# A mixed attention and state-space encoder on one core: the last pass of a score tile, rotary query times the low part of the rotary key, on all 128 rows in place of 64

## The chip, the core and the metric

The kernel runs on one core of a Trainium2 chip. A core has five engines with queues of their own: TensorE (PE in the rows, its weight loads PEld), VectorE (DVE), ScalarE (ACT), GpSimd (POOL) and SyncE (SP), which here issues all DMAs. The metric is device time in microseconds (us) of one execution, the median of several.

## The reference

Two post-norm layers over 512 tokens of width 1024. The even layer has a convolution branch, a latent attention with 8 heads and a cross-attention into 256 memory tokens; the odd layer has a bidirectional state-space branch and the same cross-attention. The change lies in the scores of the latent attention: each head has 128 plain channels and 64 rotary ones, and the rotary key is shared by all heads.

```python
def mla_block_attention(q_nope, q_rope, k_nope, k_rope, v):
    scale = (QK_NOPE + QK_ROPE) ** -0.5
    ...
        s = (jnp.einsum('bqhd,bkhd->bhqk', qn_b, k_nope).astype(jnp.float32)
             + jnp.einsum('bqhr,bkr->bhqk', qr_b, k_rope).astype(jnp.float32)) * scale
        p = jax.nn.softmax(s, axis=-1).astype(v.dtype)
        return jnp.einsum('bhqk,bkhd->bqhd', p, v)
```

## The kernel before, in words

Matrix products run in fp32r. To keep the accuracy of fp32, every operand is split into a high part (a cast to fp32r on ScalarE) and a low part (operand minus high part, on VectorE), and a product is the sum of three passes on TensorE: high times high, low times high, high times low. The helper `split_into` makes the two parts, `mm3` issues the passes.

The kernel is not written in the order in which it runs. The functions record every operation through one helper (so nearly all instructions have line 535 in the profile, and the tile names tell them apart: `sr` holds fp32r tiles in SBUF, `sb` and `sz` fp32 ones, `ps` is PSUM, `scr` is scratch in DRAM). A list scheduler then sets a fixed order for each engine, with a cost table of its own: priorities follow the recorded order, and work marked as background (the 31 taps of the convolution on VectorE, the preparation of the state-space parameters on GpSimd, VectorE and TensorE) is put into gaps. Each engine runs its order strictly, and waits on semaphores where an operand or a buffer isn't ready.

A head of the latent attention, `mla_head(h)`: it splits the weights, makes the key (`kh`, `kl`) and the query (`qh`, `ql`), and for each pair of heads the rotary query. That one is stacked: the tile `st` of a head holds in 64 rows the high part and in the other 64 rows the low part. The shared rotary key (`krh`, `krl`) stands twice in its tile, in rows 0 to 63 and again in 64 to 127, so one pass of `st` times `krh` on 128 rows gives high times high plus low times high. For each of four score tiles (128 queries by 512 keys, one PSUM bank `s`) there are five passes: three for the plain channels, one with `krh`, one with `krl`. VectorE takes the row maximum (`reduce_max`), ScalarE the exponential with the row sum, VectorE the reciprocal, ScalarE the scaling; TensorE transposes the probabilities, ScalarE and VectorE split them, and TensorE multiplies them with the values. With 8 heads there are 32 score tiles.

Around the heads the order on TensorE mixes in passes of other projections and small products of the state-space preparation, on VectorE the taps of the convolution. Behind the heads come the output projection (weights `wo`), and then the odd layer.

Of the kernel before, what the change touches and what calls it, by code (L numbers as in the profile page):

```python
# [537 lines left out]
class Kernel:  # L538
# [361 lines left out]
    def mla_head(self, h):  # L900
        nc, A = self.nc, self.A
        if h % 4 == 0:
            self.v = self.mla_v(h // 4)
        wkn = self.wload(A["wkn"][h], 256, tag="k")
        ckv = [(t[0][:], t[1][:]) for t in self.ckv]
        cqa = lambda k: (self.cq[k][0][:], self.cq[k][1][:])
        ps = self.bank("A")
        self.mm3(ps[:], [self.wk(wkn, k) for k in range(2)], ckv)
        kh, kl = self.split(ps[:])
        ps = self.projF(A["wqn"][h], cqa, 6)  # L910
        qh, ql = self.split(ps[:])
        if h % 2 == 0:
            ps = self.projF(A["wqr"][h // 2], cqa, 6)
            r = self.rope(ps)
            self.stk = []
            for i in range(2):
                st = self.big(F32R)
                a, b = slice(i * 64, i * 64 + 64), slice((1 - i) * 64, (1 - i) * 64 + 64)
                nc.scalar.copy(st[a], r[a])
                nc.vector.tensor_tensor(st[b], r[a], st[a].bitcast(F32), op=ALU.subtract)  # L920
                self.stk.append(st)
        i = h % 2
        st = self.stk[i]
        rows = slice(i * 64, i * 64 + 64)
        scale = 192.0 ** -0.5
        pr = []
        for t in range(4):
            sl = slice(t * P, (t + 1) * P)
            s = self.bank("S")
            nc.tensor.matmul(s[:], lhsT=qh[:, sl], rhs=kh[:], start=True, stop=False)  # L930
            nc.tensor.matmul(s[:], lhsT=ql[:, sl], rhs=kh[:], start=False, stop=False)
            nc.tensor.matmul(s[:], lhsT=qh[:, sl], rhs=kl[:], start=False, stop=False)
            nc.tensor.matmul(s[:], lhsT=st[:, sl], rhs=self.krh[:], start=False, stop=False)
            nc.tensor.matmul(s[:], lhsT=st[rows, sl], rhs=self.krl[rows], start=False, stop=True)
            mx = self.sm(1, tag="mx")
            nc.vector.reduce_max(mx[:], s[:], axis=AX.X)
            p = self.big(F32, "pr")
            self.softmax_tail(s[:], p[:], scale, mx[:])
            pr.append(p)
        pt = []  # L940
        for k in range(4):
            tp = self.bank("T")
            for t in range(4):
                nc.tensor.transpose(tp[:, t * P:(t + 1) * P], pr[t][:, k * P:(k + 1) * P], self.ident[:])
            pt.append(self.split(tp[:]))
        o = self.bank("V")
        vs = slice((h % 4) * P, (h % 4) * P + P)
        self.mm3(o[:], [(v[0][:, vs], v[1][:, vs]) for v in self.v], [(a[:], b[:]) for a, b in pt])
        m = self.tmp()
        nc.sync.dma_start(out=m[:], in_=self.mgd[h][:])  # L950
        nc.vector.scalar_tensor_tensor(m[:], o[:], 0.5, m[:], op0=ALU.mult, op1=ALU.mult)
        return m
# [671 lines left out]
```

## Time and profile before

| | |
|---|---|
| timed runs, us | 1058.15, 1063.86, 1064.89; median 1063.86 |
| profiled execution, us | 1060.0 |
| its span, first to last instruction, us | 1058.2 |
| busy us: TensorE, VectorE, ScalarE, GpSimd | 1007.6, 799.2, 450.1, 514.7 |
| mean granted TensorE clock | 0.979 |

The profiled execution lies among the timed ones, so its durations can be used as they are. Matmuls overlap in the rows: the duration of one is longer than the step to the next.

### The profile page before, as it was taken

To read this page: it belongs to the slowest core of one execution; us is meant where nothing else is said; L and a number is where in the kernel's file an instruction comes from. 1 tells how busy PE (TensorE), PEld (TensorE's weight loads), DVE (VectorE), ACT (ScalarE), POOL (GpSimd) and SP (SyncE) were. 2 spreads that over 40 slices of the span, in tenths; PEclk is the share of its full clock that TensorE was granted. 3 is DMA by queue.
4 is the path that set the end of the run, shared out by engine and by line. 5 is a ranking of instruction groups with operands and counts; after the bars stand their busy time and mean duration, and the time that the engine had idled before them with its cause. 6 is when DMAs were issued, how large, how long until landed. Compare 5 with 4: busy or idle time off the path is not lost. (4 is left out here: it accounts for less than half of the span.)

```text
span 1058.2 us, 15020 instructions
## 1 busy us (share of the span) xinstructions
PE 1007.6 (95%) x5296; PEld 792.2 (75%) x5296; DVE 799.2 (76%) x1285; ACT 450.1 (43%) x798; POOL 514.7 (49%) x741
## 2 busy tenths in 40 slices
PE   9999899999999999998799999999989979999996
PEld 7888788787788666665578888887767757888885
DVE  7787999999999898987896648517797695434346
ACT  5532455555323457475672223423436344422210
POOL 0557767788899988888699901000121011000001
PEclk9999999999999999998899999999999998999998
DMA  7433634325776454445398753883856633243413
GB/s 261 140 116 114 209 115 168 127 95 173 261 234 220 132 169 135 133 139 197 130 307 257 248 194 120 308 268 120 242 188 198 242 107 104 96 139 120 149 50 79
DMA packets 80171, 180.02 MB, mean 170 GB/s; under 512 B 24161, under 2 KB 28897, under 8 KB 80097
## 3 DMA queue, kind: packets, MB, share of 16 engines
q1 hardware_dynamic: 80096, 179.07, 51.9%
q8 instruction: 41, 0.67, 0.3%
q14 instruction: 34, 0.27, 0.1%
HBM read 142.93 MB, written 36.11 MB: 169 GB/s over the span
## 5 line engine op out<-in xcount | busy, mean ns | idle before, releaser
L535 PE MATMUL ps<-sr 128*128 128x512 f32 (+1 forms) x3904 | 925.5, 392 | 28.4 <-DVE sr L535 13.0
L535 PEld LDWEIGHTS ps<-sr 128*128 128x128 f32 x3904 | 709.9, 190 | 201.3 <-issue 21.7
L535 DVE TENSOR_TENSOR sr<-sb,sr 128x1024 fp32r<-128x1024 f32 (+4 forms) x230 | 270.1, 1186 | 172.4 <-ACT sr L535 130.2
L535 POOL TENSOR_TENSOR sb<-sb 128x512 f32<-128x512 f32 (+3 forms) x246 | 256.2, 1055 | 190.9 <-DVE sb L535 177.7
L535 ACT CAST sr<-sb 128x1024 fp32r<-128x1024 f32 (+4 forms) x230 | 200.7, 886 | 323.9 <-PE ps L535 187.2
L535 DVE SCALAR_TENSOR_TENSOR ps<-sb,sz,ps 128x503 f32<-128x503 f32 (+14 forms) x240 | 167.5, 736 | 0.0
L535 POOL TENSOR_TENSOR sz<-sz 128x64 f32<-128x64 f32 (+2 forms) x75 | 44.4, 596 | 221.6 <-DVE sz L535 218.2
L535 POOL TENSOR_TENSOR sb<-sb,sz 128x512 f32<-128x512 f32 (+4 forms) x160 | 131.8, 842 | 31.1 <-DVE sz L535 11.2
L535 ACT CAST sr<-ps 128x512 fp32r<-128x512 f32 (+1 forms) x100 | 55.8, 570 | 45.5 <-PE ps L535 45.2
L535 DVE TENSOR_TENSOR sr<-ps,sr 128x512 fp32r<-128x512 f32 (+1 forms) x100 | 65.3, 661 | 10.7 <-ACT sr L535 9.8
L535 ACT COPY sb<-ps 128x512 f32<-128x512 f32 (+3 forms) x78 | 40.8, 541 | 73.0 <-PE ps L535 51.9
L535 DVE SCALAR_TENSOR_TENSOR sb<-sb,ps 128x512 f32<-128x512 f32 x64 | 47.1, 739 | 29.6 <-ACT sb L535 12.5
L535 PE MATMUL ps<-sz,sb 128*128 128x128 f32 (+2 forms) x608 | 62.4, 237 | 4.1 <-DVE sr L535 1.8
L535 PE MATMUL ps<-sb 128*64 128x128 f32 (+2 forms) x768 | 58.4, 306 | 8.0 <-POOL sb L535 7.5
L535 PEld LDWEIGHTS ps<-sz,sb 128*128 128x128 f32 (+1 forms) x608 | 47.1, 131 | 20.8 <-ACT sb L535 6.8
L535 PEld LDWEIGHTS ps<-sb 128*64 128x64 f32 (+1 forms) x768 | 36.4, 131 | 33.3 <-POOL sb L535 13.1
L535 POOL TENSOR_TENSOR sb<-sz 64x64 f32<-64x64 f32 (+1 forms) x128 | 55.3, 440 | 4.9
L535 ACT ACTIVATE sb<-ps 128x512 f32<-128x512 f32 (+1 forms) x72 | 38.1, 548 | 41.1 <-PE ps L535 38.8
L535 ACT ACTIVATE sb<-ps,sz 128x256 f32<-128x256 f32 (+1 forms) x64 | 36.8, 580 | 18.6 <-DVE sz L535 13.6
L535 DVE TENSOR_TENSOR sb<-sb,ps 128x512 f32<-128x512 f32 x63 | 40.4, 680 | 2.0 <-PE ps L535 1.3
L535 DVE TENSOR_TENSOR_SCAN ps<-sb,ps 64x511 f32<-64x511 f32 x32 | 39.2, 1224 | 1.8 <-ACT ps L535 1.1
L535 ACT ACTIVATE sb<-sb,sz 128x512 f32<-128x512 f32 (+1 forms) x65 | 38.2, 622 | 5.3 <-DVE sz L535 5.2
(47 smaller groups left out, 338.9 us busy)
## 6 DMA issues: line engine op xcount, KB each, us to landing
sb<-w SPq DMA_DIRECT2D x70, 512.0 KB
sb<-scr SPq DMA_DIRECT2D x48, 512.0 KB
scr<-sb SPq DMA_DIRECT2D x40, 512.0 KB
sb<-scr SPq DMA_DIRECT2D x76, 256.0 KB
sb<-wo SPq DMA_DIRECT2D x32, 512.0 KB
scr<-sb SPq DMA_DIRECT2D x46, 256.0 KB
sb<-s5bt SPq DMA_DIRECT2D x16, 512.0 KB
sb<-wglu SPq DMA_DIRECT2D x16, 512.0 KB
```

Of the source, the lines that this page charges most:

```text
L535: o.ins = getattr(eng[o.eng], o.meth)(*[real(x) for x in o.a], **{k: real(v) for k, v in o.k.items()})
```

## The change

The fifth pass of a score tile took 64 rows of the rotary query, those that hold the high part (rows 0 to 63 for an even head, 64 to 127 for an odd one), and the same rows of `krl`. Now it takes all 128 rows of both, so the low part of the rotary query times the low part of the rotary key is added to the score: a product that was left out before. The fourth and the fifth pass now have the same stationary tile. The number of instructions and their order on each engine are the same in both kernels; 32 matmuls and their 32 weight loads have another shape.

```diff
         i = h % 2
         st = self.stk[i]
-        rows = slice(i * 64, i * 64 + 64)
...
             nc.tensor.matmul(s[:], lhsT=st[:, sl], rhs=self.krh[:], start=False, stop=False)
-            nc.tensor.matmul(s[:], lhsT=st[rows, sl], rhs=self.krl[rows], start=False, stop=True)
+            nc.tensor.matmul(s[:], lhsT=st[:, sl], rhs=self.krl[:], start=False, stop=True)
```

## Rows read from the trace of the kernel before

**Rows 1.** The page, part 1 and the granted clock of part 2
```profile
PE 1007.6 (95%) x5296; PEld 792.2 (75%) x5296; DVE 799.2 (76%) x1285; ACT 450.1 (43%) x798; POOL 514.7 (49%) x741
PEclk9999999999999999998899999999999998999998
```

**Rows 2.** Chain of waits: start us, us, what; its longest piece
```profile
875.05 174.04 PE ps L535 x794
```

**Rows 3.** PE by shape, whole span: busy us, mean ns, idle before
```profile
L535 PE MATMUL ps<-sr 128*128 128x512 f32 x3584 | 877.6, 399 | 26.8 <-DVE sr L535 11.8 <-DVE sb L535 7.1 <-ACT sb L535 4.5
L535 PE MATMUL ps<-sr 64*128 64x512 f32 x32 | 17.3, 542 | 0.0
```

**Rows 4.** Windows: busy us of PE, PEld, DVE, ACT, POOL, clock, DMA
```profile
345.00:553.00 208.00, 187.75 (x993) 130.31 (x992) 180.96 (x306) 126.77 (x246) 177.31 (x223) 0.95 0.51 166
553.00:1058.20 505.20, 484.06 (x2624) 388.71 (x2623) 302.06 (x401) 173.51 (x305) 86.99 (x91) 0.98 0.53 171
```

**Rows 5.** Waits of PE, 355 to 553 us: us, times, longest
```profile
PE ps L535 <- DVE sr L535: 8.7, 10, 2.2
PE ps L535 <- DVE sb L535: 7.1, 3, 3.4
```

**Rows 6.** Timeline of PE: start us, us, matmuls merged, [idle before them]
```profile
355.57 2.21 PE L535 MATMUL ps<-sr 128*128 128x512 f32 x5 [0.89 <-DVE sr L535]
557.77 11.52 PE L535 MATMUL ps<-sr 128*128 128x512 f32 x50
```

**Rows 7.** PE by shape, inside the first row of rows 6 alone
```profile
L535 PE MATMUL ps<-sr 64*128 64x512 f32 x2 | 1.0, 493 | 0.0
```

**Rows 8.** 64-row matmuls in the stretches of rows 10 to 14, in order
```profile
L535 PE MATMUL ps<-sr 64*128 64x512 f32 x4 | 2.0, 495 | 0.0
L535 PE MATMUL ps<-sr 64*128 64x512 f32 x7 | 3.5, 497 | 0.0
L535 PE MATMUL ps<-sr 64*128 64x512 f32 x4 | 2.0, 497 | 0.0
L535 PE MATMUL ps<-sr 64*128 64x512 f32 x3 | 2.4, 791 | 0.0
L535 PE MATMUL ps<-sr 64*128 64x512 f32 x2 | 1.3, 642 | 0.0
```

**Rows 9.** Timeline of PE while the granted clock is 0.50
```profile
496.62 2.96 PE L535 MATMUL ps<-sr 128*128 128x512 f32 x4
```

**Rows 10.** Waits of DVE, 357.9 to 370.6 us
```profile
DVE sz L535 <- PE ps L535: 1.7, 3, 0.8
DVE sz L535 <- ACT sz L535: 0.4, 1, 0.4
DVE sr L535 <- ACT sr L535: 0.3, 1, 0.3
```

**Rows 11.** Waits of DVE, 387.0 to 411.4 us
```profile
DVE sz L535 <- PE ps L535: 1.5, 3, 0.9
DVE sz L535 <- ACT sz L535: 0.7, 1, 0.7
```

**Rows 12.** Waits of DVE, 454.4 to 479.5 us
```profile
DVE sz L535 <- PE ps L535: 1.5, 1, 1.5
```

**Rows 13.** Waits of DVE, 495.3 to 504.8 us
```profile
DVE sr L535 <- PE ps L535: 2.8, 1, 2.8
```

**Rows 14.** Waits of DVE, 517.8 to 552.8 us
```profile
DVE sr L535 <- ACT sr L535: 2.2, 4, 1.0
DVE sb L535 <- PE ps L535: 0.7, 1, 0.7
```

**Rows 15.** Timeline of PE, after the passes of 506 to 508 us
```profile
513.15 2.80 PE L535 MATMUL ps<-sr 128*128 128x512 f32 x5 [3.38 <-DVE sb L535]
```

**Rows 16.** DVE by shape, 345 to 553 us, with and without a PSUM operand
```profile
L535 DVE TENSOR_TENSOR sr<-ps,sr 128x512 fp32r<-128x512 f32 x51 | 34.3, 682 | 5.8 <-ACT sr L535 5.6
L535 DVE TENSOR_TENSOR sr<-sz,sr 128x256 fp32r<-128x256 f32 x6 | 10.0, 1660 | 0.0
```

## The prediction

> **What bounds the kernel now.** Page first: TensorE is busy 95% of the span, VectorE 76% [rows 1]. The chain of waits is all TensorE from 875 us on [rows 2]. The edited pass runs elsewhere, so the by-shape list comes next: the 32 passes on 64 rows are the group 64*128; one lasts 542 ns, a 128-row pass of the same 512 columns 399 ns [rows 3]. Asked for 355 to 553 us alone, the view gives the same row of 32: they all lie in the attention stage. The window of 345 to 553 us shows what holds there. Of its 208 us TensorE is busy 187.75, VectorE 180.96 and GpSimd 177.31 [rows 4]: three engines within 5% of each other, handing work back and forth. TensorE waits 8.7 + 7.1 us there for VectorE [rows 5]. Behind 553 us TensorE is busy 484 of 505 us, and VectorE (302) and GpSimd (87) have room [rows 4]. So what TensorE gains by 553 us should reach the end whole, and the question is how much of its saving survives the attention stage.
>
> **What the change removes and adds.** It removes 32 passes on 64 rows and adds 32 on 128 rows with the same 512 columns. No instruction is added or moved, no wait is new (the pass before already reads all rows of both the query tile and the high key tile; the low key tile is finished in all 128 rows with the krl that the old pass read), and no DMA differs.
>
> Price of one pass. Durations overlap, so I use the step from one matmul to the next. A plain run of 128-row passes: 50 in 11.52 us, less about 0.40 for the last one's own time [rows 3], is 11.12 / 49 = 0.227 us a step [rows 6]. The run of five at 355.57 us holds two 64-row passes [rows 7] in second and fourth place, so each of its four steps goes from one number of rows to the other: (2.21 - 0.49) / 4 = 0.43 us a step [rows 6, 7]. Each change of rows costs 0.43 - 0.227 = 0.20 us, on the way in and on the way out, and a 64-row pass between two 128-row passes 0.40 us. So the dear thing is not the pass but the two edges around it, and the edit takes both edges away; the pass itself is priced like any other. Five of the 32 run while the granted clock is 0.50: the three that last 791 ns, one of the two with a mean of 642 ns [rows 8], and one of those that I set to 0 below. There, four matmuls in alternation take 2.96 us [rows 9], a step of (2.96 - 0.79) / 3 = 0.72 us, 0.79 being the last one's own time; a plain step at half the clock is no more than twice 0.227, so an edge costs at least 0.27 us and such a pass 0.54 us.
>
> TensorE's own saving: 27 x 0.40 + 5 x 0.54 = 13.5 us, or 1.3% of the run. The new pass has a row to go by (0.227 us a step), so its price is not open; how much arrives is.
>
> **What arrives.** I cut the stage at the places where TensorE stands idle for another engine. A saving ahead of such a place counts only if the engine that ends the wait is earlier too, and VectorE, with its fixed order, gets earlier only by what it had itself waited for TensorE (or for ScalarE behind TensorE) in that stretch. So each stretch passes on the smaller of two numbers:
>
> 355.57 to 370.6 us: six passes, two [rows 7] and four [rows 8], save 2.4 us; VectorE waited 1.7 + 0.4 + 0.3 us [rows 10]. Passes 2.4.
>
> 387 to 411.4 us: seven passes save 2.8 us [rows 8]; VectorE waited 1.5 + 0.7 us [rows 11]. Passes 2.2.
>
> 454.4 to 479.5 us: four save 1.6 us [rows 8]; the row maximum waited 1.5 us for its scores [rows 12]. Passes 1.5.
>
> 495.3 to 504.8 us: three, at half the clock, save 1.6 us [rows 8]; VectorE waited 2.8 us [rows 13]. Passes 1.6.
>
> 517.8 to 552.8 us: two save 0.9 us [rows 8]; VectorE waited 0.7 us for TensorE, and 2.2 us for ScalarE, of which I can't say how much is TensorE's [rows 14]. Passes 0.7.
>
> The other ten (32 less 22) save 4.1 us, which I set to 0 between bounds of 0 and 4.1: ahead of 513.15 us, for one, TensorE stands idle 3.38 us for a VectorE product [rows 15], and being there sooner only lengthens that wait. Sum: 2.4 + 2.2 + 1.5 + 1.6 + 0.7 = 8.4 us.
>
> One term has either sign. VectorE and GpSimd slow each other when both read SBUF: a difference with 256 columns and no PSUM operand takes 1660 ns in this stage, one with 512 columns from PSUM 682 ns [rows 16]. Six such cost about 6 us more than they would alone; if TensorE comes sooner, which of VectorE's work falls beside which of GpSimd's is dealt anew. A fifth of 6 us either way, 1.2 us, is my bound; I take 0.
>
> The profiled execution took 1060.0 us (span 1058.2 and 1.8 around it), so its counterpart takes 1060.0 - 8.4 = 1051.6 us. It was among the quicker: the three timed runs span 1058.15 to 1064.89 us, median 1063.86. Against that median the forecast is 1063.9 - 8.4 = 1055.5 us, 0.8% faster. About 1% is what a measurement of this kernel can tell from no change.
>
> **Rivals.** All of it arrives. If VectorE's waits for ScalarE and the waits that I set to 0 give way as well, 13.5 us come through: 1050.4 us. For it: VectorE is idle 27 us of the 208 [rows 4], twice the saving. Against it: TensorE's own 15.8 us of waiting for VectorE [rows 5] is time in which it is not the late one.
>
> Little of it arrives. My sums assume that several short waits in a row can all be used up. If only the stretches count in which one long wait of VectorE for TensorE stands behind the passes [rows 12, 13, 14], it is 1.5 + 1.6 + 0.7 = 3.8 us: 1060.1 us. For it: VectorE and GpSimd are nearly as full as TensorE [rows 4].
>
> Slower than before, by the clock. Where TensorE waits it loses its clock: the slices from 476 to 529 us show 0.8 [rows 1], and the stage has a mean of 0.95 [rows 4]. The change makes TensorE wait longer for VectorE by what doesn't arrive, 13.5 - 8.4 = 5.1 us. At half the clock a plain step takes up to 0.45 in place of 0.227 us, so each microsecond at 0.50 on full work loses half a microsecond. The run comes out slower than before once 2 x 8.4 = 17 us more of such time fall on work that sets the end; with 30 us more it is 15 - 8.4 = 6.6 us slower, 1070.5 us. Against it: the stage has 0.05 x 208 / 0.5 = 21 us of such time now [rows 4], and a third more waiting (15.8 to 21 us) adds, in proportion, 7 us of it, not 17. The Trainium skill, TensorE: Matmul & The Clock Gate, section HAM oscillation, says that gaps in TensorE's work bring the throttled clock back; by that rule the longer waits would cost something, and the lowered clock of these slices agrees.
>
> The price is not what the rows say. If a 64-row pass were dear for something that stays (it is the last of its sum, and it loads the query tile a second time), nothing would change: 1063.9 us. Against it: the step out of a 64-row pass, which belongs to the next matmul, is as dear as the step in [rows 6, 7]. The same page of the Trainium skill, section Why this matters for your kernels, says that a single matmul on few rows takes the time of one on 128, the gain being only in running several side by side; by that rule the edit is free and useless. The trace differs: 542 against 399 ns [rows 3].
>
> **How the numbers follow.** Forecast (6 to 10.5 us arrive): 0.47, 1053.4 to 1057.9 us. All arrives: 0.21. Little arrives: 0.22. Clock: 0.05. No change: 0.05. The predicted time is the likeliest case's, 1055.5 us. The range goes from 1049.5 us (all of it, and 1 us for the dealing of VectorE's work) to 1061.5 us (little of it, and the same); it leaves out the last two cases and some scatter of the medians. Faster by over 1% means under 1053.2 us: most of the second case and a tenth beside it, 0.29. Slower by over 1% takes the clock case at its worst: 0.03. Within 1%: 0.68.
>
> **What would show it.** In the changed profile the group 64*128 is gone, and the 128-row group has 3616 passes with a mean under 399 ns; no run of 128-row passes in the attention stage has steps of 0.43 us. VectorE's row maxima wait less for TensorE at 360 to 370, 400 to 410 and 461 us, and TensorE waits longer for VectorE than 15.8 us in the stage. Behind it the kernel is the same, some 8 us earlier. I am wrong if the run of TensorE behind 553 us doesn't keep the lead (a wait for a weight load would show it), if the stage's clock falls well under 0.95, or if the 64-row edges were covered by waits that the trace puts elsewhere.

## The result and the profile after

The changed kernel takes 1054.35 us (median of 9 runs, 1053.0 to 1057.88), the kernel before 1062.1 (9 runs, 1058.15 to 1064.89). The ratio is 0.993 with a 95% interval of 0.9911 to 0.9948, so the gain is 7.75 us by the medians and 5.5 to 9.5 us by the interval (1062 x 0.0052 and x 0.0089). The forecast was 8.4. The profiled execution took 1053.0 us with a span of 1051.2, against 1060.0 and 1058.2; a pair of single executions, whose difference of 7.0 us is read below.

The page, part 1, after the change, which answers to [rows 1]; the row of the granted clock is the same as there:

```profile
PE 996.0 (95%) x5296; PEld 793.0 (75%) x5296; DVE 798.4 (76%) x1285; ACT 449.7 (43%) x798; POOL 513.9 (49%) x741
```

TensorE is busy 11.6 us less than in [rows 1] (996.0 against 1007.6) with the same count, and the other three by less than 1 us. By shape (busy us, mean ns of one, idle before), the group 64*128 of [rows 3] is gone, and its 32 passes are in the group of 128 rows, at its mean:

```profile
L535 PE MATMUL ps<-sr 128*128 128x512 f32 x3616 | 880.1, 398 | 28.1 <-DVE sr L535 12.1 <-DVE sb L535 6.6 <-ACT sb L535 6.5
```

The edges themselves are seen in TensorE's timeline, in the five matmuls that answer to the first of [rows 6]:

```profile
354.56 1.43 PE L535 MATMUL ps<-sr 128*128 128x512 f32 x5 [0.90 <-DVE sr L535]
```

They took 2.21 us and now 1.43, 0.78 us less for four edges, 0.195 each on average. From start to start the last three steps are now 0.233 to 0.236 us, where they were 0.42 to 0.43; the first, behind the wait, is 0.335 and was 0.43.

The windows (busy us of TensorE, its weight loads, VectorE, ScalarE, GpSimd, then clock and DMA), cut at the same instructions as [rows 4]:

```profile
345.00:545.60 200.60, 174.91 (x988) 128.95 (x986) 178.79 (x303) 126.68 (x246) 175.47 (x221) 0.96 0.53 170
545.60:1051.20 505.60, 484.04 (x2624) 388.65 (x2624) 302.40 (x402) 173.25 (x305) 87.51 (x92) 0.98 0.54 171
```

Behind the attention stage nothing has changed: 484.04 against 484.06 us of TensorE in 505.6 against 505.2 us. The longest piece of the chain of waits (start us, us) is that of [rows 2], 6.75 us earlier:

```profile
868.30 173.76 PE ps L535 x794
```

The clock has a part in the gain that the prediction did not count. The stage's granted clock is 0.96 against 0.95; by the trace that is 17.0 us at 0.50 in place of 20.4, and at most half of the difference, 1.7 us, is time gained. Over the nine runs the mean is 0.979, and 0.976 over the 51 runs of the kernel before that stand beside the experiments: 0.003 of 1060 us is some 3 us. Up to that much of the 7.75 us may be clock, whether by the change or by chance; no run here separates it.

In the stage VectorE (178.79 us) and GpSimd (175.47) are now as busy as TensorE (174.91), which led before. The waits agree; TensorE's and then VectorE's, from 355 us to the stage's end (us, times, longest):

```profile
PE ps L535 <- DVE sr L535: 9.0, 11, 2.2
PE ps L535 <- ACT sb L535: 7.6, 5, 2.6
PE ps L535 <- DVE sb L535: 6.6, 3, 4.1
```

```profile
DVE sr L535 <- ACT sr L535: 6.8, 10, 2.4
DVE sz L535 <- PE ps L535: 2.1, 5, 0.6
DVE sr L535 <- PE ps L535: 1.6, 3, 1.2
```

TensorE waits for VectorE 15.6 us, as in [rows 5], and for ScalarE 7.6 us, where before it was 3.0 us in 4 waits. VectorE waits for TensorE's scores (`sz`) 2.1 us where it waited 7.1 us (12 times, longest 1.5), and with `sr` 1.6 where it was 3.6. So VectorE's slack behind TensorE, which the prediction spent stretch by stretch, was indeed used up. The longest of its waits for ScalarE's casts, 2.4 us, is met again below.

**Where the 7 us of the pair arose.** The order is the same in both kernels, so each matmul of one has its counterpart. How much earlier it starts in the changed kernel, by its time in the kernel before:

| at, us | 110 | 120 | 345 | 370 | 387 | 410 | 440 | 450 | 480 | 500 | 530 | 550 | end |
|---|---|---|---|---|---|---|---|---|---|---|---|---|---|
| earlier by, us | -0.07 | 1.21 | 1.02 | 2.82 | 1.19 | 2.45 | 2.83 | 3.72 | 4.36 | 6.15 | 6.59 | 6.9 | 7.02 |

1.0 us was there at 345 us, ahead of the first changed pass, so it is scatter between executions. The stage adds 5.9 us, the rest of the run 0.1. Within the stage the lead grows along the edited passes and falls at waits. At 451.55 us TensorE's wait for ScalarE grows from 0.35 to 1.57 us, and the 1.2 us gained since 440 us are gone again. Between 505 and 518 us 0.9 us are lost on balance, to a wait for ScalarE (1.78, now 2.58 us) and to the wait of [rows 15], which is now:

```profile
506.90 2.50 PE L535 MATMUL ps<-sr 128*128 128x512 f32 x5 [4.05 <-DVE sb L535]
```

The largest loss is 1.6 us between 370 and 387 us. These are the lines of VectorE, ScalarE and SyncE's queue there, first of the kernel before, then of the changed one:

```profile
378.30 0.73 SPq L535 DMA_DIRECT2D sz<-wkn  x1
381.66 1.37 DVE L535 SCALAR_TENSOR_TENSOR ps<-sb,sz,ps 128x497 f32<-128x497 f32 x2
381.80 0.40 ACT L535 CAST sr<-sz 128x256 fp32r<-128x256 f32 x1
382.94 3.24 DVE L535 TENSOR_TENSOR sr<-sz,sr 128x256 fp32r<-128x256 f32 x1
```

```profile
377.15 0.73 SPq L535 DMA_DIRECT2D sz<-wkn  x1
378.84 1.37 DVE L535 SCALAR_TENSOR_TENSOR ps<-sb,sz,ps 128x497 f32<-128x497 f32 x2
382.22 0.41 ACT L535 CAST sr<-sz 128x256 fp32r<-128x256 f32 x1 [3.13 <-DMA sz<-wkn]
382.65 2.35 DVE L535 TENSOR_TENSOR sr<-sz,sr 128x256 fp32r<-128x256 f32 x1 [2.44 <-ACT sr L535]
```

VectorE reaches its two taps (the second line of each) 2.82 us earlier. The load of the next key weights, `wkn`, is issued only 1.15 us earlier, and the cast of it comes 5.07 us after the issue in place of 3.50. ScalarE now stands 3.13 us for that load and VectorE 2.44 us for ScalarE. TensorE waits 2.51 us for ScalarE there. VectorE's product is done 1.18 us earlier (385.00 against 386.18), and this is what is left of the lead. Why the issue is only 1.15 us earlier is in the waits of SyncE's queue from 370 to 384 us, before and then after:

```profile
SPq L535 <- POOL sz L535: 8.3, 1, 8.3
```

```profile
SPq L535 <- POOL sz L535: 8.2, 1, 8.2
```

The load stands in its queue behind a transfer that waits 8 us for GpSimd, and GpSimd's part came only 1.15 us earlier, little more than the 1.0 us that were there at 345 us. This is a reading of the rows; it was not tried by itself.

### The profile page after: what moved, and what is told of

Same layout as the page of the kernel before. It is cut to its first block, busy times and chain, and to the rows that moved or that the text cites. A ratio compares the mean times of both kernels' runs of the same rounds, so it can differ in the third digit from the quotient of the medians.

```text
span 1051.2 us, 15020 instructions
## 1 busy us (share of the span) xinstructions
PE 996.0 (95%) x5296; PEld 793.0 (75%) x5296; DVE 798.4 (76%) x1285; ACT 449.7 (43%) x798; POOL 513.9 (49%) x741
## 5 line engine op out<-in xcount | busy, mean ns | idle before, releaser
L535 PE MATMUL ps<-sr 128*128 128x512 f32 (+1 forms) x3904 | 914.1, 390 | 29.7 <-DVE sr L535 13.3
L535 PEld LDWEIGHTS ps<-sr 128*128 128x128 f32 x3904 | 710.1, 190 | 189.4 <-DVE sr L535 19.6
L535 DVE TENSOR_TENSOR sr<-sb,sr 128x1024 fp32r<-128x1024 f32 (+4 forms) x230 | 269.1, 1181 | 170.6 <-ACT sr L535 135.0
L535 POOL TENSOR_TENSOR sb<-sb 128x512 f32<-128x512 f32 (+3 forms) x246 | 256.1, 1055 | 192.4 <-DVE sb L535 178.2
L535 ACT CAST sr<-sb 128x1024 fp32r<-128x1024 f32 (+4 forms) x230 | 200.6, 886 | 321.5 <-PE ps L535 178.8
L535 DVE SCALAR_TENSOR_TENSOR ps<-sb,sz,ps 128x503 f32<-128x503 f32 (+14 forms) x240 | 167.4, 736 | 0.0
L535 POOL TENSOR_TENSOR sz<-sz 128x64 f32<-128x64 f32 (+2 forms) x75 | 45.3, 608 | 222.3 <-DVE sz L535 218.0
L535 POOL TENSOR_TENSOR sb<-sb,sz 128x512 f32<-128x512 f32 (+4 forms) x160 | 130.1, 832 | 28.8 <-DVE sz L535 11.2
L535 ACT CAST sr<-ps 128x512 fp32r<-128x512 f32 (+1 forms) x100 | 55.8, 571 | 40.8 <-PE ps L535 39.8
L535 DVE TENSOR_TENSOR sr<-ps,sr 128x512 fp32r<-128x512 f32 (+1 forms) x100 | 65.4, 661 | 8.2 <-ACT sr L535 7.1
L535 ACT COPY sb<-ps 128x512 f32<-128x512 f32 (+3 forms) x78 | 40.8, 541 | 71.3 <-PE ps L535 51.4
L535 DVE SCALAR_TENSOR_TENSOR sb<-sb,ps 128x512 f32<-128x512 f32 x64 | 47.1, 740 | 29.6 <-ACT sb L535 12.7
L535 PE MATMUL ps<-sz,sb 128*128 128x128 f32 (+2 forms) x608 | 62.4, 237 | 6.8 <-ACT sb L535 4.1
L535 PE MATMUL ps<-sb 128*64 128x128 f32 (+2 forms) x768 | 58.4, 307 | 8.5 <-POOL sb L535 8.0
L535 PEld LDWEIGHTS ps<-sz,sb 128*128 128x128 f32 (+1 forms) x608 | 47.4, 132 | 24.2 <-ACT sb L535 10.8
L535 PEld LDWEIGHTS ps<-sb 128*64 128x64 f32 (+1 forms) x768 | 36.2, 131 | 34.0 <-POOL sb L535 13.0
L535 POOL TENSOR_TENSOR sb<-sz 64x64 f32<-64x64 f32 (+1 forms) x128 | 55.4, 441 | 4.9
L535 ACT ACTIVATE sb<-ps 128x512 f32<-128x512 f32 (+1 forms) x72 | 38.1, 548 | 41.2 <-PE ps L535 38.9
L535 ACT ACTIVATE sb<-ps,sz 128x256 f32<-128x256 f32 (+1 forms) x64 | 36.8, 580 | 20.0 <-DVE sz L535 11.6
L535 DVE TENSOR_TENSOR sb<-sb,ps 128x512 f32<-128x512 f32 x63 | 40.4, 681 | 2.1 <-PE ps L535 1.5
L535 DVE TENSOR_TENSOR_SCAN ps<-sb,ps 64x511 f32<-64x511 f32 x32 | 39.2, 1225 | 1.8 <-ACT ps L535 1.1
L535 ACT ACTIVATE sb<-sb,sz 128x512 f32<-128x512 f32 (+1 forms) x65 | 38.1, 621 | 3.7 <-DVE sz L535 3.7
```

Of the source, the lines that this page charges most:

```text
L535: o.ins = getattr(eng[o.eng], o.meth)(*[real(x) for x in o.a], **{k: real(v) for k, v in o.k.items()})
```

## The experiments

My theory: a change of row count costs 0.20 us, the edges are all that the edit removes, and the stage passes on only what VectorE had itself waited for. The rivals: the 64-row pass itself is dear; its last place is; or the missing 5 to 6 us are lost in some other way than to VectorE.

In kernels marked "same order", each engine's order is laid out for the unedited kernel, and an operation carries in `alt` what is issued in its place. Their lines read L536 or L538 in place of L535. The kernel before was run again beside each group of four: the median is 1062.94 us for the first four kernels below, 1063.6 for the two with taps and the two with fills on 64 and on 128 rows, and 1062.05 for the other four.

**Both rotary passes on 64 rows.** The kernel before, same order; the product of the query's low part with the high key is left out.

```diff
-            nc.tensor.matmul(s[:], lhsT=st[:, sl], rhs=self.krh[:], start=False, stop=False)
+            o4 = nc.tensor.matmul(s[:], lhsT=st[:, sl], rhs=self.krh[:], start=False, stop=False)
+            o4.alt = [("matmul", (s[:],), dict(lhsT=st[rows, sl], rhs=self.krh[rows], start=False, stop=False))]
```

> Fourth and fifth pass of a score tile both on 64 rows (the low query part times the high key is left out), instruction order of every engine as in the kernel before. Theory (the price sits in the two edges where the number of rows changes, 0.2 us each): still two edges a tile, so the step inside the pair is 0.23 us and the time is that of the kernel before, 1062 us within 3. Rival (a 64-row pass itself is dear by 0.4 us): TensorE has 12.8 us more to do and the run comes out 6 to 10 us above the kernel before, 1068 to 1072 us.

Measured: 1058.75 us, ratio 0.9963 (0.9944 to 0.9981). By shape:

```profile
L536 PE MATMUL ps<-sr 64*128 64x512 f32 x64 | 23.8, 457 | 0.0
```

Twice as many 64-row passes, and the kernel did not get slower; it came out just under the range that I had given. The mean of one fell from the 542 ns of [rows 3] to 457, because half of them follow another. The step inside a pair is not the 0.23 us that I expected: behind a change of rows it is 0.33 to 0.34 us at the full clock, and it is 0.229 to 0.240 only where the 64-row pass ahead follows another one. The step before a change, among plain passes, is 0.32 us. So an edge takes about 0.1 us ahead of the change and 0.1 behind it, 0.20 together, and 64-row passes among themselves have plain steps. The pass on 64 rows is not dear, and the rival falls. That the kernel got 4 us faster is more than four edges fewer explain (60 in place of 64, 0.8 us). In the profiled pair the spans are equal (1058.3 and 1058.2), and where those 4 us come from stays open; the runs' mean clock, 0.978 against 0.976, is worth up to 2 of them.

**Sixty-four edges where nothing else is late.** The changed kernel, with 32 passes of the odd layer's gated projection on 64 rows: two of the 24 of each of 16 products, which lose half of those sums.

```diff
         for n, (l, r) in enumerate(seq):
+            if n in half:
+                l, r = l[0:64], r[0:64]
...
-        self.mm3(ps[:, :n], [self.wk(w, k) for k in range(kt)], [act(k) for k in range(kt)], kfirst=kfirst)
+        self.mm3(ps[:, :n], [self.wk(w, k) for k in range(kt)], [act(k) for k in range(kt)], kfirst=kfirst, half=half)
...
-        pa = self.projF(A["wglu"][2 * c], zact, 8)
-        pg = self.projF(A["wglu"][2 * c + 1], zact, 8)
+        pa = self.projF(A["wglu"][2 * c], zact, 8, half=(2, 5))
+        pg = self.projF(A["wglu"][2 * c + 1], zact, 8, half=(2, 5))
```

> The changed kernel with 32 of the 128-row passes of the last gated projection put on 64 rows (the other 64 rows of these passes are left out), each between two 128-row passes, in the stretch behind 870 us where the chain is TensorE alone; order of all engines unchanged. Theory: 64 edges at 0.20 us, nothing hides them, so 12.8 us come through whole: 1054.4 + 12.8 = 1067.2 us, range 1065 to 1069. Rival (the price belongs to the last pass of a score tile): no change, 1054.4 us.

Measured: 1070.12 us, ratio 1.0054 (1.0033 to 1.0076), 15.8 us above the changed kernel and above my range. By shape, and the longest piece of the chain of waits:

```profile
L535 PE MATMUL ps<-sr 64*128 64x512 f32 x32 | 15.9, 498 | 0.0
```

```profile
875.28 185.15 PE ps L535 x794
```

The same 794 instructions take 185.15 us, against 173.76. Instruction by instruction, this kernel is 6.0 us behind the changed one at 880 us and 18.4 at 980: 12.4 us for 64 edges, 0.194 each. This is the price of the prediction, in a place where all of it arrives. The 6 us ahead of that (some 3 by the medians) arose before any edited pass; the trace has further stretches at a granted clock of 0.50, at 428 and 766 to 773 us among others (the runs' mean is 0.977 against 0.979 for the changed kernel, worth up to some 2 us), and I can't say what brought them.

**No fifth pass.** The changed kernel, same order, with the low key's product left out, so that TensorE has 32 x 0.227 = 7.3 us less.

```diff
-            nc.tensor.matmul(s[:], lhsT=st[:, sl], rhs=self.krh[:], start=False, stop=False)
-            nc.tensor.matmul(s[:], lhsT=st[:, sl], rhs=self.krl[:], start=False, stop=True)
+            o4 = nc.tensor.matmul(s[:], lhsT=st[:, sl], rhs=self.krh[:], start=False, stop=False)
+            o5 = nc.tensor.matmul(s[:], lhsT=st[:, sl], rhs=self.krl[:], start=False, stop=True)
+            o4.alt, o5.alt = [("matmul", o4.a, dict(o4.k, stop=True))], []
```

> The changed kernel without the fifth pass (query times low key is left out), order of all engines otherwise pinned. TensorE saves 32 x 0.227 = 7.3 us more than in the changed kernel. Theory (VectorE withholds part of a saving in the attention stage, some 0.6 of it arrives): 4 to 5 us under the changed kernel, 1050 us. Rival 'all arrives': 1047 us. Rival 'little arrives': 1053 us or more.

Measured: 1055.71 us, ratio 0.9928 (0.991 to 0.9946): the same as the changed kernel. My 4 to 5 us fell. TensorE's waits from 345 to 553 us, and the stage's window:

```profile
PE ps L536 <- ACT sb L536: 10.5, 10, 2.7
PE ps L536 <- DVE sr L536: 8.6, 9, 2.2
```

```profile
345.00:545.60 200.60, 173.34 (x961) 126.35 (x959) 178.80 (x305) 126.63 (x246) 174.73 (x221) 0.93 0.53 169
```

It now waits 10.5 us for ScalarE's probabilities, in 10 waits, and stretches at the half clock (granted 0.50, which is 1.2 GHz) appear at 385.6 and 450.4 us that the changed kernel doesn't have. With 7.3 us of work gone, TensorE's busy time in the stage fell by only 1.6 us (173.34 against 174.91): most of the saving went into the clock, 0.93 against 0.96, and not into idle time. By the trace that is 27.3 us at 0.50 against 17.0, and up to half of the difference, 5 us, is time lost. Whether the saving itself lowered the clock is not shown: the six runs have a mean of 0.978 against 0.979, worth up to 2 us.

**The fifth pass twice.** The changed kernel, same order, with that product counted twice.

```diff
+            o5.alt = [("matmul", o5.a, dict(o5.k, stop=False)), ("matmul", o5.a, o5.k)]
```

> The changed kernel with the fifth pass issued twice (the term with the low key is added twice), order pinned: 7.3 us more on TensorE, no edges. Theory (VectorE is as late as TensorE in part of the stage): 4 to 6 us above the changed kernel, 1058.5 to 1060.5 us. Rival 'TensorE is the only bound': 7.3 us above, 1061.7 us. Rival 'VectorE sets the stage': 2 us above or less.

Measured: 1060.64 us, ratio 0.9988 (0.9972 to 1.0005), 6.3 us above the changed kernel for 7.3 us of added work, between my 4 to 6 us and the rival's 7.3. In its profiled run about 4 us of that arose in the stage, and some 3 more behind 600 us, where a stretch at 0.50 stands at 662.8 us that the changed kernel doesn't have. VectorE's waits from 345 to 553 us have its wait for the scores back:

```profile
DVE sz L536 <- PE ps L536: 5.9, 11, 1.2
```

Taken together: from the changed kernel, more work on TensorE costs half of its time or more, and less brings nothing. That fits a stage at the corner at which TensorE stops being the late engine, but since the clock fell as work was taken out, the corner is not shown.

**A lighter VectorE.** Every second convolution tap left out (112 instructions), same order, with the fifth pass on 64 rows, on 128, and left out as above.

```diff
-            nc.vector.scalar_tensor_tensor(acc[:, lo:hi], g[:, lo + d:hi + d], w(j), acc[:, lo:hi],
+            o = nc.vector.scalar_tensor_tensor(acc[:, lo:hi], g[:, lo + d:hi + d], w(j), acc[:, lo:hi],
...
+            if j % 2:
+                o.alt = []
```

> The kernel before (fifth pass on 64 rows) with every second convolution tap left out on VectorE (112 taps of 0.735 us, 82 us of its work, about a third of it in the attention stage), order pinned. It is the base for the next run; by itself it should be faster than the kernel before, since TensorE's 16 us of waits for VectorE in the stage shrink: 1035 to 1050 us.

> The same with the fifth pass on 128 rows; half the taps left out, order pinned. Theory (VectorE's work in the stage is what withholds the rest of the 13.5 us): with room on VectorE the difference to the run on 64 rows grows from 7.8 us to 11 to 13.5 us. Rival (what withholds it is the chain of short hand-overs between TensorE, ScalarE and VectorE, whatever VectorE's load, or the clock): the difference stays at 6 to 9 us.

> Half the convolution taps left out and the fifth pass left out, order pinned: 7.3 us less on TensorE than the run with half the taps and the pass on 128 rows (1050.1 us). Theory (VectorE's load holds the stage at the changed kernel's pace): 3 us or more arrive, 1047 us or less. Rival (GpSimd or the hand-overs hold it): under 2 us, 1048.5 to 1051 us.

Measured: 1061.01 us (0.9942 to 0.9991 of before), 1050.14 (0.9833 to 0.9914) and 1045.0 (0.9815 to 0.9879). With 59 us less of VectorE's work in the kernel the old passes gained 2.6 us, far from what I had expected: most of the taps' time is not on the path. The windows of the first (columns as above) show VectorE idle for 40 us of these 208, and TensorE busier than in [rows 4], at a lower clock (0.93 against 0.95):

```profile
345.00:553.00 208.00, 190.31 (x1017) 132.69 (x1017) 168.25 (x285) 127.71 (x249) 179.61 (x224) 0.93 0.53 170
```

But the step to 128 rows gained 10.9 us here against 7.75, just under the 11 to 13.5 us of my theory, and leaving the pass out 5.1 more (2.9 by the ratios, each to the kernel before that ran beside it), against nothing. Both point to VectorE as one of what withholds the rest. The intervals overlap (by the ratios the step is 9.8 us, with some 5 either way, and the clock, 0.980 against 0.978, can be 2 of it), so neither is shown by itself.

**A GpSimd that doesn't read.** The 208 wide GpSimd products of the state-space preparation replaced by fills with zero, same order, with the same three forms of the fifth pass.

```diff
+        if eng == "POOL" and meth == "tensor_tensor" and o.bg and outs[0].n >= 512:
+            o.alt = [("memset", (outs[0], 0.0), {})]
```

> The kernel before (fifth pass on 64 rows) with 208 wide products of the state-space preparation on GpSimd replaced by memsets (their arithmetic is left out), order pinned: GpSimd reads no SBUF beside VectorE there. Base for the next run; faster than the kernel before by what VectorE loses beside GpSimd on the path, 5 to 20 us.

> The same with the fifth pass on 128 rows, GpSimd's 208 wide products again memsets. Theory (VectorE's own work withholds the saving, GpSimd only through VectorE): with VectorE some 10 us lighter the difference to the run on 64 rows is a little above 7.8 us, 8 to 11 us. Rival (the dealing of VectorE's and GpSimd's reads is the main thing): 12 us or more. Rival (neither matters): 6 to 8 us.

> GpSimd's 208 wide products as memsets and the fifth pass left out, order pinned: 7.3 us less on TensorE than the run with memsets and the pass on 128 rows (1038.9 us). Theory (GpSimd's reads beside VectorE are what let nothing more through when the pass was left out of the changed kernel): now 3 us or more arrive, 1036 us or less. Rival (the hand-overs between TensorE, ScalarE and VectorE hold the stage, GpSimd or not): under 2 us, 1037 to 1040 us.

Measured: 1045.78 us (0.9785 to 0.9864 of before), 1038.85 (0.9717 to 0.9789) and 1035.65 (0.9722 to 0.9785). The kernel with the old passes becomes 17.8 us faster, and the step to 128 rows brings 6.9 us, as in the full kernel. GpSimd's products cost much, but no sign is seen that they hold back this change; with some 5 us either way the step could still hide one. The last step brings 3.2 us by the medians and none by the ratios: not settled. VectorE's differences by shape, 300 to 560 us, in the first of the three:

```profile
L538 DVE TENSOR_TENSOR sr<-sz,sr 128x256 fp32r<-128x256 f32 x7 | 2.9, 418 | 0.0
```

418 ns, where [rows 16] has 1660 and the same window of the kernel before 1483 (7 of them). The Trainium skill, SBUF — State Buffer, section Who interferes with whom, says that a VectorE instruction with two SBUF inputs contends with a GpSimd instruction that reads SBUF and not with one that only writes; this agrees with it.

**96 rows.** The kernel before, with the fifth pass of the even heads on 96 rows and of the odd ones on 128; a single execution.

```diff
-        rows = slice(i * 64, i * 64 + 64)
+        rows = slice(0, 96 if i == 0 else 128)
```

> The fifth pass on 96 rows for even heads, on 128 for odd ones (32 low rows of the even heads' query are left out), order as in the changed kernel. If any pass on fewer rows has edges, the 16 passes on 96 rows show steps of 0.43 us in and out; if 96 rows are run like 128, they show 0.23 us and the span is that of the changed kernel within 3 us.

Measured: 1058.07 us. This one run says little, since the 64 matmuls ahead of the stage that began at 335.14 us in the kernel before began at 340.43 here. The rows say more: by shape, and the five matmuls of [rows 6] again, now with two passes on 96 rows:

```profile
L535 PE MATMUL ps<-sr 96*128 96x512 f32 x16 | 6.6, 410 | 0.0
```

```profile
360.50 1.45 PE L535 MATMUL ps<-sr 128*128 128x512 f32 x5 [0.89 <-DVE sr L535]
```

1.45 us, as with 128 rows (1.43) and not as with 64 (2.21), and from start to start the steps from 96 rows to 128 and back are 0.225 to 0.241 us wherever the passes stand among plain ones: from 96 to 128 rows there is no edge.

**Less of the preparation in the stage.** The changed kernel, with the last 6 of the 25 pieces of the state-space preparation held back until the seventh head is recorded; the order is new.

```diff
-                self.bg(self.s5_prep(), res=RESERVEP, POOL=50000, DVE=PREP)
+                self.prep = self.s5_prep()
+                self.bg(self.prep, 19, res=RESERVEP, POOL=50000, DVE=PREP)
...
+        if self.gate is not None:
+            o.preds[self.gate] = 1
...
+            if h == 6:
+                nc.gate = nc.ops[-1]
+                self.bg(self.prep, res=RESERVEP, POOL=50000, DVE=PREP)
+                nc.gate = None
```

> The changed kernel with the last six of the 25 pieces of the state-space preparation held back until the seventh head is recorded; the scheduler lays out a new order. Theory (GpSimd beside VectorE costs time in the attention stage, 17.8 us in all by the memset run, and VectorE has room behind 553 us): a few us faster than the changed kernel, 1048 to 1053 us. Rival (the new order brings waits of its own, or TensorE's small products of the preparation are as dear later): no faster, 1054 us or more.

Measured: 1050.97 us, ratio 0.9876 (0.9839 to 0.9913), 3.4 us under the changed kernel by the medians; the two intervals just touch. One of its six runs took 1967 us for a reason that I don't know, and is not in the ratio. Its windows:

```profile
345.00:545.60 200.60, 180.25 (x960) 134.03 (x959) 178.63 (x311) 129.45 (x251) 121.30 (x149) 0.98 0.47 155
545.60:1050.00 504.40, 479.30 (x2659) 381.93 (x2657) 309.28 (x395) 169.80 (x301) 151.16 (x165) 0.99 0.55 178
```

GpSimd has 121 us of work in the stage in place of 175, the clock is 0.98, and the 64 us that moved behind the stage cost little there. The five runs have a granted clock of 0.985 to 0.990, the changed kernel's nine 0.974 to 0.983, so the clock alone is enough for the 3.4 us; that it is GpSimd's reads is not shown.

## Why the prediction was right

**What bounds the kernel.** Held: the stage ahead of 553 us decides, and what TensorE has gained by then reaches the end whole (6.9 us earlier at 550 us, 7.02 at the end).

**The price.** Held: 0.20 us an edge was worked out, 0.195 is seen in the row after, and 0.194 was measured in another stage. The edges are the cause, not the pass (64 passes on 64 rows, with 60 edges, cost no more) and not its last place in the sum, which it still has. Not every edge is at the full price where small matmuls stand beside it: the 19 matmuls at 358.17 us, the first of them on 64 rows, took 5.00 us and now take 4.90. The sum of 13.5 us was thus too high: TensorE's busy time fell by 11.6 us, and added up from start to start over the steps into, at and out of the 32 passes the saving is some 12 us (one step into a wait left out). At the half clock a step with an edge is 0.72 us and a plain one 0.43 in the changed kernel, 0.30 for the edge, where at least 0.27 was forecast. The Trainium skill, TensorEngine Tiling (Array Packing), section Key Properties, says that a change of the tiling mode drains TensorE. The edges agree with that, and the 96 rows agree with the same page's list of row tilings (section Available Configurations), which has 128, 64 and 32. The other page that the prediction weighed, the Trainium skill, TensorE: Matmul & The Clock Gate, section Why this matters for your kernels (a single matmul on few rows takes the time of one on 128), held for the pass (64-row passes among themselves have plain steps). That the edit is useless does not follow from it here, because of the edges.

**What arrives.** Held in the sum, 7.75 against 8.4 us, and less well in the terms. (The predicted 1055.5 us went from 1063.86 us, the median of three runs; over nine it is 1062.1.) In the profiled pair:

| stretch, us | forecast | came |
|---|---|---|
| 355.57 to 370.6 | 2.4 | 1.8 |
| 370.6 to 387 | 0 | -1.6 |
| 387 to 411.4 | 2.2 | 1.7 |
| 454.4 to 479.5 | 1.5 | 1.5 |
| 495.3 to 504.8 | 1.6 | 2.5 |
| 517.8 to 552.8 | 0.7 | 1.1 |
| the rest of the stage | 0 | -1.1 |
| sum | 8.4 | 5.9 |

The worst-sized terms are those that I put at 0 between bounds of 0 and the saving. Both came out below nothing, because a lead in hand can be lost again at a later wait: in the second stretch ScalarE ran into a load whose queue is held by GpSimd, and in the rest the 0.9 us of 505 to 518 us were lost, with 0.2 us at 485 us. What the terms passed on elsewhere is nearer, and in 495.3 to 504.8 us more than forecast; the kernel before ran there for 6.8 us at the half clock and the changed one for 3.4 us, so a part of it may be clock. VectorE's product in the second stretch took 2.35 us in place of 3.24: the term of either sign (1.2 us) shows in it, and here it helped.

So the pair's 5.9 us in the stage are 2.5 us under the forecast, and that the medians come within 0.7 us of it is in part luck: misses of either sign, and the clock. One sign that I gave failed: TensorE was to wait longer for VectorE than 15.8 us. It waits 15.6, and what doesn't arrive stands in its waits for ScalarE, 7.6 us in place of 3.0.

**The rivals.** That all arrives is refuted for this kernel; with half the taps gone 10.9 us came, near the whole, but the interval there is wide. That little arrives (3.8 us) lies outside the interval; of the kernel's next step, the pass left out, nothing arrived. The clock did not fall with the change (0.96 against 0.95 in the stage), but it did in the profiled run with the pass left out (0.93), so this rival was not idle. What divides the withheld 4 to 6 us among VectorE's work, ScalarE's hand-overs, late loads and the clock stays open.

## What to carry to other kernels

In a stream of matmuls on 128 rows, price a pass on 64 rows by the steps around it, not by its rows: filling it up to 128 rows with duplicated or useful data can be faster than leaving rows out. Count what a faster engine gains only as far as the engines behind it had waited for it, look in each stretch for a load whose queue waits for a third engine, and let a term that you put at 0 go below it. Adding the work once and taking it out once tells how near a stage is to hanging on another engine, if the granted clock of the runs is set beside their times.

## What the hardware showed that I had not expected

64 rows beside 128 cost 0.20 us at each change, half of it on the step ahead and half on the step behind, and 96 beside 128 nothing. A VectorE difference of 256 columns took 1660 ns on average beside GpSimd's products and 418 ns beside its fills. The kernel with the fills was 17.8 us faster, more than the change studied; how much of that is VectorE's and how much GpSimd's own shorter work is not separated. Half of the taps taken off VectorE was worth 2.6 us.
